# Token sums of the seven-product channel mixer made per token tile in the output stage, second weight's rows loaded ahead of hidden group 0

## The chip, the cores and the metric

The kernel runs on one core of one Trainium2 chip. The metric is the device time of one execution in microseconds (us); the kernel before took 1729.72 us (median of three runs, 1728.2 to 1732.3).

## What is computed

One layer of a decoder: a normalised and modulated input goes through one wide projection, two kinds of attention, two up projections that are merged by gates, an output projection with a residual, and then a channel mixer. The change lies in the last two parts. S = 1024 tokens, D = 1024 channels, FF = 4096 hidden units, all in float32:

```
mixed = (sigmoid(m_a) * y_a + sigmoid(m_b) * y_b) @ w_out
h  = h + gate1 * mixed
u2 = rms_norm(h, norm2_g) * (1 + scale2) + shift2
ff = square(relu(u2 @ mlp_w1)) @ mlp_w2
h  = h + gate2 * ff
```

## The kernel before

Every float32 product is made as three products of parts: an operand x is split into a high part (`hi`, line 61, a cast on ScalarE) and the rest (`lo`, line 66, a subtraction on VectorE or GpSimd), and TensorE sums high by high, high by low and low by high. A matmul takes a 128x128 stationary part and 512 moving columns.

**The output stage** (lines 1431 to 1487) goes over eight token tiles t of 128 tokens. `out_mm(t, dh)` makes one half of a tile's 1024 channels with 24 matmuls (line 1441), and VectorE multiplies by the gate row and adds to `acc` (lines 1443, 1444); ScalarE sums squares (1445). `norm2` makes the scale and the normalised tile `hn` (1449, 71 to 75, 1452). `turn2` transposes it (1460, eight pieces of 128 columns), modulates it on ScalarE into `uf` (1463, eight pieces), writes `uf` to DRAM (`u_d`, 1465), and splits it into the mixer's input `mth` and `mtl` (1467, 1468). These two tiles are called `u2h` and `u2l` in the mixer; index 0 holds tokens 0 to 511, index 1 the rest.

**The channel mixer** goes over eight groups of 512 hidden units. Group 0's hidden units are made plainly by `hidden_units(0)`: eight units of 24 matmuls each (line 1525), of which those for th = 1 read the tokens of index 1. Groups 1 to 7 use Strassen's form with seven products instead of eight for both of the mixer's matmuls. `first_units(c)` makes the hidden units of group c by seven products n = 0 to 6 of 24 matmuls each (line 1638); n = 0 and 1 read `u2h[0]` and `u2l[0]`, the five others read a sum of token blocks. These sums T0 to T4 (high and low part, 1 MB each) lie in DRAM as `t_d`, and `stream` (1572) loads them for each group into a `ring` of two slots, which are the two halves of `u2h[1]` and `u2l[1]`. Slot 0 and slot 1 are free once `hidden_units(0)` has read its last unit.

The sums are made by `token_sums`, a generator which `hidden_units(0)` drives one step per unit: it loads four blocks of `u_d` per step (1542), makes t1 (VectorE, 1550), t3 (GpSimd, 1551), t2 (VectorE, 1552) and t4 (GpSimd, 1553), splits the four results (four casts at 61, four subtractions at 66, two of them on each engine), and writes eight parts to `t_d` (1560). Its fifth sum is the plain block (1534, 1535).

`product(c, m)` makes the second matmul's product m of group c from sums of hidden units and sums of `mlp_w2` blocks (lines 1675 to 1684; sums of raw blocks and the second weight's low parts on GpSimd), 24 matmuls at line 1701, and adds into `acc` (1704). Before that, `w2_load` loads four 512 KB rows of `mlp_w2` (1662) and multiplies them by the gate row `grow2` on GpSimd (1663). For group 0 this stands after unit 5 of `hidden_units`, when the sums' pool `tp` has been closed and the pool `mw`, which holds `w2` and the operands, has been opened in its place:

```
        if n == 5:
            gate_row(grow2, 3, 5 * D, px)
            for _ in sums:
                pass
            close(tp)
            mw = pool("mw", "left")
            w2_load(0)
```

All DMAs of these stages are issued by SP, in the order in which they stand. Each engine executes its list in order; a scheduler of the framework has set each list's order from the program, so that work of neighbouring steps is interleaved. `first_units(c + 1)` is interleaved with the seven products of group c.

Of the kernel before, what the change touches and what calls it, by code (L numbers as in the profile page):

```python
# [35 lines left out]
def build(tc, I, out):  # L36
# [49 lines left out]
    oa_d = dr.tile([512, S], F32, name="oa_d")  # L86
    ob_d = dr.tile([512, S], F32, name="ob_d")
    acc_d = dr.tile([4, 128, D], F32, name="acc_d")
    u_d = dr.tile([NK, 128, S], F32, name="u_d")
    t_d = dr.tile([5, 2, 128, 2048], F32, name="t_d")  # L90

    ps = pool("ps", space=PSUM)
# [1362 lines left out]
    def turn2(t, hn):  # L1455
        uf = t4.tile([128, NK, 128], F32, name="uf4", bufs=2)
        for q in range(2):
            p = px()
            for k in range(4):
                nc.tensor.transpose(p[:, k * 128:(k + 1) * 128], hn[:, (q * 4 + k) * 128:(q * 4 + k + 1) * 128], ident)  # L1460
            for k in range(4):
                kk = q * 4 + k
                nc.scalar.activation(uf[:, kk], p[:, k * 128:(k + 1) * 128], AF.Identity,
                                     scale=a2[:, kk:kk + 1], bias=s2[:, kk:kk + 1])
        nc.sync.dma_start(u_d[:, :, t * 128:(t + 1) * 128].rearrange("k p t -> p k t"), uf)
        ts_ = slice((t % 4) * 128, (t % 4 + 1) * 128)
        nc.vector.tensor_copy(u2h[t // 4][:, :, ts_], uf)
        nc.vector.tensor_tensor(u2l[t // 4][:, :, ts_], uf, f(u2h[t // 4])[:, :, ts_], op=OP.subtract)

    u2h, u2l = mth, mtl  # L1470
    wq = pool("wq", "right")
    for t in range(4):
        out_mm(t, 0)
    wo_s[1] = [out_w(k, 1, wq, 4) for k in range(4)]
    late = []
    for t in range(NT):
        if t >= 4:
            out_mm(t, 0)
        out_mm(t, 1)
        late.append((t, norm2(t)))  # L1480
        while len(late) > (2 if t < 4 else 1):
            turn2(*late.pop(0))
    turn2(*late.pop(0))
    close(wq)
    close(gt)
# [10 lines left out]
    w2k = I["mlp_w2"][0]  # L1496
    CH = 4
    NC = FF // 128 // CH
    grow2 = ml.tile([128, D], F32, name="grow2")


    PRODUCTS = (
        (((1, 0, 0),), ((1, 0, 1), (-1, 1, 1)), ((1, 0, 1), (1, 1, 1))),
# [24 lines left out]
            nc.scalar.activation(r, r, AF.Square)  # L1528
            yield


    def token_sums(tp):

        nc.sync.dma_start(t_d[4, 0], f(u2h[1])[:, 4:].rearrange("p k t -> p (k t)"))
        nc.sync.dma_start(t_d[4, 1], f(u2l[1])[:, 4:].rearrange("p k t -> p (k t)"))

        def load(kk):
            X = {}
            for th in range(2):
                for j in range(2):  # L1540
                    X[j, th] = tp.tile([128, 512], F32, name="x%d%d" % (j, th), bufs=2)
                    nc.sync.dma_start(X[j, th], u_d[4 * j + kk][:, th * 512:(th + 1) * 512])
            return X

        X = {kk: load(kk) for kk in range(2)}
        yield
        for kk in range(4):
            b11, b12, b21, b22 = (X[kk][i] for i in ((0, 0), (0, 1), (1, 0), (1, 1)))
            t1 = tp.tile([128, 512], F32, name="t1", bufs=2)
            nc.vector.tensor_tensor(t1, b12, b11, op=OP.subtract)  # L1550
            nc.gpsimd.tensor_tensor(b12, b22, b12, op=OP.subtract)
            nc.vector.tensor_tensor(b22, b22, t1, op=OP.subtract)
            nc.gpsimd.tensor_tensor(b21, b21, b22, op=OP.subtract)
            for n, (src, e) in enumerate(((b22, "v"), (b12, "g"), (b21, "g"), (t1, "v"))):
                h = tp.tile([128, 512], F32R, name="th", bufs=7)
                l = tp.tile([128, 512], F32R, name="tl", bufs=7)
                hi(h, src, "s")
                lo(l, src, h, e)
                for q, t_ in enumerate((h, l)):
                    nc.sync.dma_start(t_d[n, q][:, kk * 512:(kk + 1) * 512], f(t_))  # L1560
            yield
            if kk + 2 < 4:
                X[kk + 2] = load(kk + 2)

    ring = [(u2h[1][:, q * 4:q * 4 + 4], u2l[1][:, q * 4:q * 4 + 4]) for q in range(2)]
    streams = [(c, n) for c in range(1, NC) for n in range(5)]
# [45 lines left out]
    def first_units(c):  # L1612
# [10 lines left out]
        for n in range(7):  # L1623
            a_prep(*((c, n + 1) if n < 6 else (c + 1, 0)))
            wh, wl = SPL.pop((c, n))
            q = (c - 1) * 5 + n - 2
            bh, bl = (u2h[0][:, n * 4:n * 4 + 4], u2l[0][:, n * 4:n * 4 + 4]) if n < 2 else ring[q % 2]
            if n == 0:
                R = [pd(), pd()]
            if n in (1, 5):  # L1630
                B = [pt(), pt()]
            bank = R if n in (0, 2, 3, 4) else B
            on = n in (2, 3, 4, 6)
            for ft in range(2):
                fs = slice(ft * 128, (ft + 1) * 128)
                for k in range(4):
                    for m, (a, b) in enumerate(((wh, bh), (wh, bl), (wl, bh))):
                        nc.tensor.matmul(bank[ft], a[:, k, fs], b[:, k], start=(k == 0 and m == 0 and not on),  # L1638
                                         stop=(k == 3 and m == 2), skip_group_check=on)
                if n in (0, 2, 3):  # L1640
                    t = r_tile()
                    nc.scalar.copy(t, bank[ft])
                    (c11, None, u2_, u3_)[n].append(t)
                elif n == 4:
                    t = H[c][2 + ft, 0] = r_tile()
                    act(t, bank[ft])
                else:
                    t = {1: c11, 5: u3_, 6: u2_}[n][ft]
                    nc.vector.tensor_tensor(t, t, bank[ft], op=OP.add)
                    act(t, t)  # L1650
                    H[c][{1: (ft, 0), 5: (2 + ft, 1), 6: (ft, 1)}[n]] = t
            if n >= 2:
                stream(q + 2)
            if 3 <= n < 6:
                a_load(c + 1, n - 3)
            yield

    def w2_load(c, js=range(4)):

        for j in js:  # L1660
            t = W2[c][j] = mw.tile([128, D], F32, name="w2", bufs=4)
            nc.sync.dma_start(t, w2k[(c * CH + j) * 128:(c * CH + j + 1) * 128, :])
            nc.gpsimd.tensor_tensor(t, t, grow2, op=OP.mult)  # L1663

    def side_of(terms, block, name, e):

        h = mw.tile([128, 2, 512], F32R, name=name + "h", bufs=2)
        l = mw.tile([128, 2, 512], F32R, name=name + "l", bufs=2)
        if len(terms) == 2:
            (_, i0, j0), (sg, i1, j1) = terms  # L1670
            src = wr.tile([128, D], F32, name="raw", bufs=3)
# [37 lines left out]
    ORDER = (0, 3, 2, 4, 5, 1, 6)  # L1709
    LAST = {(i, j): m for m in ORDER for _, i, j in PRODUCTS[m][2]}  # L1710
    H, W2 = [{} for _ in range(NC)], [{} for _ in range(NC)]
    tp = pool("tp", "left")
    sums = token_sums(tp)
    for n, _ in enumerate(hidden_units(0)):
        next(sums, None)
        if n in (1, 2, 3):
            a_load(1, n - 1)
        if n == 5:
            gate_row(grow2, 3, 5 * D, px)
            for _ in sums:  # L1720
                pass
            close(tp)
            mw = pool("mw", "left")
            w2_load(0)
    a_prep(1, 0)
    for q in range(2):
        stream(q)
    for c in range(NC):
# [3 lines left out]
        for n, m in enumerate(seq):  # L1732
# [3 lines left out]
                ops = operands(c, seq[n + 1])  # L1736
            if n in (4, 5) and c + 1 < NC:
                w2_load(c + 1, range(2 * n - 8, 2 * n - 6))
            product(c, m, cur)
        next(nxt, None)  # L1740
    finish()
# [23 lines left out]
```

## Time and profile before

| What | us |
|---|---|
| median of three runs | 1729.72 |
| profiled execution, whole | 1733.76 |
| its span in the trace | 1732.0 |
| TensorE (PE) busy | 1650.1 |
| VectorE (DVE) busy | 1270.9 |
| GpSimd (POOL) busy | 946.9 |
| ScalarE (ACT) busy | 876.5 |

PE is the busiest engine. A time such as 1127 in this text is microseconds from the span's start. The output stage's matmuls run from 975 to 1068, group 0's hidden units from 1069 to 1116, and the Strassen form starts at 1116. A matmul's listed duration overlaps its neighbour's; what one costs in a row is read from the starts of successive ones.

### The profile page before, as it was taken

What the parts mean: (1) busy time and instruction counts of PE and PEld (TensorE: products, weight loads), DVE (VectorE), ACT (ScalarE), POOL (GpSimd) and SP (SyncE); (2) the same over time, 40 slices, a digit from 0 to 9 for tenths busy, and PEclk for the clock granted to TensorE, in tenths of its full rate; (3) what the DMA queues carried; (4) which work ended last, traced back from release to release, by engine and by line L of the source; (5) the groups of instructions that cost most, each with busy time, mean ns of one, the idle gap of its engine ahead of it and who ended that gap; (6) DMA issues with size and microseconds to landing.
All of it is one profiled execution on the core that took longest, in us unless ns stands there. A gap on an engine that the chain in (4) does not pass through costs nothing.

```text
span 1732.0 us, 25317 instructions
## 1 busy us (share of the span) xinstructions
PE 1650.1 (95%) x8484; PEld 1386.7 (80%) x8484; DVE 1270.9 (73%) x2614; ACT 876.5 (51%) x1898; POOL 946.9 (55%) x837
## 2 busy tenths in 40 slices
PE   5999999999999989999999999949999999999998
PEld 4879888888888867778778888837788888888886
DVE  7598478777777557778564555737898888979887
ACT  6433366666666456766454344524444444444442
POOL 0021143333433377865145200659998898979897
PEclk9999999999999989999999999969999999999999
DMA  9365312111211164441286523974263645637232
GB/s 306 100 181 168 104 47 59 52 54 49 62 48 44 37 194 128 135 110 47 75 299 226 200 81 109 339 304 159 75 266 134 255 154 199 223 118 279 98 146 97
DMA packets 164922, 249.42 MB, mean 144 GB/s; under 512 B 15592, under 2 KB 113592, under 8 KB 155576
## 3 DMA queue, kind: packets, MB, share of 16 engines
q1 hardware_dynamic: 160568, 245.71, 42.7%
q10 hardware_dynamic: 4224, 2.10, 0.4%
q8 instruction: 67, 1.10, 0.3%
q14 instruction: 63, 0.52, 0.1%
HBM read 205.81 MB, written 41.96 MB: 143 GB/s over the span
## 4 chain that ended last, share of the span: by engine, by line
PE 75%; POOL 7%; DMA 6%; DVE 5%; ACT 3%; issue 2%; SPq 1%; POOLq 0%; DVEq 0%; ACTq 0%
PE pd L748 16%; PE psx L1701 10%; PE pd L1638 7%; PE pt L1638 5%; PE px L1441 5%; PE px L1329 5%; PE po L913 4%; PE pt L947 4%; POOL raw L1675 3%; PE po L1701 3%; DMA adraw<-in_ada_w_dram 2%; PE psx L829 2%; PE psx L830 2%; PE px L1525 2%; PE cb L304 1%
## 5 line engine op out<-in xcount | busy, mean ns | idle before, releaser
L1704 DVE TENSOR_TENSOR acc<-acc,psx 128x512 f32<-128x512 f32 x288 | 178.6, 675 | 16.5 <-PE psx L1701 16.2
L748 PE MATMUL pd<-uh,uwh 128*128 128x512 f32 x448 | 181.6, 405 | 0.7 <-ACT zo L1023 0.7
L748 PE MATMUL pd<-ul,uwh 128*128 128x512 f32 x448 | 178.0, 397 | 0.0
L748 PE MATMUL pd<-uh,uwl 128*128 128x512 f32 x448 | 176.9, 395 | 0.0
L66 DVE TENSOR_TENSOR wl<-aw,wh 128x1024 fp32r<-128x1024 f32 x49 | 107.0, 2184 | 75.2 <-ACT wh L61 75.2
L1675 POOL TENSOR_TENSOR raw<-r 128x512 f32<-128x512 f32 x80 | 135.1, 1708 | 26.8 <-ACT r L1616 26.7
L1701 PE MATMUL psx<-wbl,rah 128*128 128x512 f32 x336 | 131.6, 392 | 5.7 <-POOL wbl L1677 4.3
L1701 PE MATMUL psx<-wbh,rah 128*128 128x512 f32 x336 | 130.6, 391 | 1.3 <-DVE acc L1704 1.3
L1701 PE MATMUL psx<-wbh,ral 128*128 128x512 f32 x336 | 130.8, 389 | 0.0
L905 DVE TENSOR_TENSOR tl<-pt,th 128x512 fp32r<-128x512 f32 (+8 forms) x168 | 103.6, 619 | 34.5 <-ACT th L904 33.4
L904 ACT CAST th<-pt 128x512 fp32r<-128x512 f32 (+8 forms) x168 | 88.7, 530 | 60.8 <-PE pt L947 58.8
L1677 POOL TENSOR_TENSOR wbl<-raw,wbh 128x1024 fp32r<-128x1024 f32 x40 | 105.7, 2643 | 18.9 <-ACT wbh L1676 18.9
L886 POOL TENSOR_TENSOR pcx<-pcx,tot 128x64 f32<-128x64 f32 (+7 forms) x32 | 10.5, 329 | 172.2 <-DVE tot L884 95.3
L1663 POOL TENSOR_TENSOR w<-w,grow 128x1024 f32<-128x1024 f32 x32 | 91.9, 2894 | 17.8 <-DMA w<-in_mlp_w_dram 17.8
L63 POOL TENSOR_SCALAR uwh<-uwr 128x512 fp32r<-128x512 f32 x54 | 33.5, 629 | 123.3 <-PE pd L748 96.8
L748 PEld LDWEIGHTS pd<-uh,uwl 128*128 128x128 f32 x448 | 85.0, 190 | 17.8
L1638 PE MATMUL pd<-mth,wh 128*128 128x512 f32 x224 | 88.6, 397 | 9.3 <-DMA mth<-t_d 7.7
L748 PEld LDWEIGHTS pd<-uh,uwh 128*128 128x128 f32 x448 | 85.4, 191 | 14.9 <-ACT zo L1023 1.1
L1676 ACT CAST rah<-raw 128x1024 fp32r<-128x1024 f32 x40 | 41.5, 1051 | 109.8 <-PE po L1701 61.0
L748 PEld LDWEIGHTS pd<-ul,uwh 128*128 128x128 f32 x448 | 85.3, 191 | 13.2
L1638 PE MATMUL pd<-mtl,wh 128*128 128x512 f32 x224 | 88.6, 395 | 6.2 <-DMA mtl<-t_d 6.2
L1638 PE MATMUL pd<-mth,wl 128*128 128x512 f32 x224 | 88.3, 394 | 0.0
(361 smaller groups left out, 5357.9 us busy)
## 6 DMA issues: line engine op xcount, KB each, us to landing
mth<-t_d SPq DMA_DIRECT2D x35, 1024.0 KB, 8.0
mtl<-t_d SPq DMA_DIRECT2D x35, 1024.0 KB, 5.0
w<-in_mlp_w_dram SPq DMA_DIRECT2D x32, 512.0 KB, 6.0
z_d<-zo SPq DMA_DIRECT2D x56, 256.0 KB, 2.0
aw<-in_mlp_w_dram SPq DMA_DIRECT2D x28, 512.0 KB, 4.9
uwr<-in_w_in_dram SPq DMA_DIRECT2D x54, 256.0 KB, 3.0
adraw<-in_ada_w_dram SPq DMA_DIRECT2D x48, 256.0 KB, 3.2
xa<-in_ada_w_dram SPq DMA_DIRECT2D x32, 256.0 KB, 5.9
```

The lines of the kernel that those rows point to most:

```text
L66: (nc.vector if e == "v" else nc.gpsimd).tensor_tensor(dst, src, f(h), op=OP.subtract)
L748: r = nc.tensor.matmul(p, a, b, start=(k == 0 and n == 0), stop=(k == NK - 1 and n == 2))
L904: nc.scalar.copy(th[:rows, :w], p[:rows, :w])
L905: nc.vector.tensor_tensor(tl[:rows, :w], p[:rows, :w], f(th)[:rows, :w], op=OP.subtract)
L1329: nc.tensor.matmul(p, a, b, start=(k == 0 and n == 0), stop=(k == 3 and n == 2))
L1441: nc.tensor.matmul(p, a[:, k, ts_], b[:, k % 2], start=(k == 0 and n == 0), stop=(k == NK - 1 and n == 2))
L1638: nc.tensor.matmul(bank[ft], a[:, k, fs], b[:, k], start=(k == 0 and m == 0 and not on), stop=(k == 3 and m == 2), skip_group_check=on)
L1663: nc.gpsimd.tensor_tensor(t, t, grow2, op=OP.mult)
L1675: nc.gpsimd.tensor_tensor(d, block(i0, j0, s), block(i1, j1, s), op=OP.add if sg > 0 else OP.subtract)
L1677: (nc.vector if e == "v" else nc.gpsimd).tensor_tensor(l.rearrange("p s n -> p (s n)"), src, f(h).rearrange("p s n -> p (s n)"), op=OP.sub ...
L1701: nc.tensor.matmul(p, a[:, s, qs], b[:, s], start=(s == 0 and n == 0), stop=(s == 1 and n == 2))
L1704: nc.vector.tensor_tensor(acc[:, t, ds_], acc[:, t, ds_], p, op=OP.add if sg > 0 else OP.subtract)
```

## The change

The sums are made by blocks of 128 tokens in the output stage: pair b joins tile b (loaded back from `u_d` as one 512 KB tile `ux`, with one buffer) and tile b + 4 (just transposed and still in `uf`). `token_sums(b, ...)` is called at the end of `turn2(b + 4)`, and asks for the next pair's `ux` at its end. Only tiles 0 to 3 are written to `u_d`, in rows of 4 KB. The parts now lie in `t_d` token block by token block, so the five Strassen products that read a sum take a moving operand of four runs of 128 columns, 512 columns apart. The small tiles of the sums lie in the output stage's pool `t4`, and pools `tp` and `mw` are gone: `w2` and the operands live in `ml`. The first weight's raw blocks of group 1 and the four rows of `mlp_w2` for group 0 are asked for ahead of `hidden_units(0)`; their product with `grow2` (`w2_gate`) follows unit 2. The output weight's second half takes one tile of pool `wr`, one of `wx` and two of `wq` instead of four of `wq`.

```
-        nc.sync.dma_start(u_d[:, :, t * 128:(t + 1) * 128].rearrange("k p t -> p k t"), uf)
+        uff = uf.rearrange("p k t -> p (k t)")
+        if t < 4:
+            nc.sync.dma_start(u_d[t], uff)
...
+        if t >= 4:
+            token_sums(t - 4, uff[:, :512], uff[:, 512:])
+    def u_load(b):
+        t = uxs[b] = t4.tile([128, D], F32, name="ux", bufs=1)
+        nc.sync.dma_start(t, u_d[b])
+    def token_sums(b, b12, b22):
+        ux = uxs.pop(b)
+        b11, b21 = ux[:, :512], ux[:, 512:]
+        t1, t2, t3 = (t4.tile([128, 512], F32, name="t%d" % n, bufs=1) for n in (1, 2, 3))
+        nc.vector.tensor_tensor(t1, b12, b11, op=OP.subtract)
+        nc.gpsimd.tensor_tensor(t3, b22, b12, op=OP.subtract)
+        nc.vector.tensor_tensor(t2, b22, t1, op=OP.subtract)
+        nc.gpsimd.tensor_tensor(b21, b21, t2, op=OP.subtract)
+        for n, (src, e) in enumerate(((t2, "v"), (t3, "g"), (b21, "g"), (t1, "v"))):
...
+            hi(h, src, "s")
+            lo(l, src, h, e)
...
+        if b < 3:
+            u_load(b + 1)
-    wo_s[1] = [out_w(k, 1, wq, 4) for k in range(4)]
+    wo_s[1] = [out_w(k, 1, *((), (wx, 4), (wq, 2), (wq, 2))[k]) for k in range(4)]
...
+        if t == 4:
+            u_load(0)
...
+                bs = [[t_.rearrange("p b (k t) -> p b k t", k=4)[:, :, k] for k in range(4)] for t_ in ring[q % 2]]
...
-    tp = pool("tp", "left")
-    sums = token_sums(tp)
+    for n in range(3):
+        a_load(1, n)
+    grow2 = ml.tile([128, D], F32, name="grow2")
+    w2_load(0)
     for n, _ in enumerate(hidden_units(0)):
-        next(sums, None)
-        if n in (1, 2, 3):
-            a_load(1, n - 1)
-        if n == 5:
+        if n == 2:
             gate_row(grow2, 3, 5 * D, px)
-            for _ in sums:
-                pass
-            close(tp)
-            mw = pool("mw", "left")
-            w2_load(0)
+            w2_gate(0)
```

On SP, where group 0 ends, the list before holds the last parts' writes, then ring loads, first-weight loads (`aw`) and the rows `w2`:

```order
L1560 DMA t_d_64<-tl_13385 128x512
L1560 DMA t_d_64<-tl_13373 128x512
L1572 DMA mth1_11521<-t_d_64 128x2048
L1578 DMA aw_13806<-in_mlp_w1_dram 128x4x256
L1560 DMA t_d_64<-tl_13379 128x512
L1572 DMA mth1_11521<-t_d_64 128x2048
L1572 DMA mtl1_11523<-t_d_64 128x2048 x2
L1578 DMA aw_13808<-in_mlp_w1_dram 128x4x256
L1662 DMA w2_13432<-in_mlp_w2_dram 128x1024
L1662 DMA w2_13435<-in_mlp_w2_dram 128x1024
```

The same place after the change:

```order
L1493 DMA t_d_64<-tl_13183 128x512
L1576 DMA aw_13197<-in_mlp_w1_dram 128x4x256
L1576 DMA aw_13199<-in_mlp_w1_dram 128x4x256
L1576 DMA aw_13201<-in_mlp_w1_dram 128x4x256
L1663 DMA w2_13209<-in_mlp_w2_dram 128x1024
L1663 DMA w2_13211<-in_mlp_w2_dram 128x1024
L1663 DMA w2_13213<-in_mlp_w2_dram 128x1024
L1663 DMA w2_13215<-in_mlp_w2_dram 128x1024
L1576 DMA aw_13205<-in_mlp_w1_dram 128x4x256
L1570 DMA mtl1_11523<-t_d_64 128x2048
L1570 DMA mth1_11521<-t_d_64 128x2048
```

The rows `w2` stood behind three ring loads and now stand ahead of the first one, behind the last write of a sum.

On VectorE, from tile 5's split (`mth1`) to the low parts of hidden unit weights (`wl`), the list before:

```order
L1467 CAST mth1_11521<-uf4_12922 128x8x128
L1449 TENSOR_TENSOR rst2_111<-ssq2_110 128x1
L1468 TENSOR_TENSOR mtl1_11523<-uf4_12922,mth1_11521 128x8x128
L72 RECIPROCAL rtm_107<-rtm_107 128x1
L73 SCALAR_TENSOR_TENSOR rtm_107<-rst2_111,rtm_107 128x1
L74 SCALAR_TENSOR_TENSOR rtm_107<-rtm_107 128x1
L75 SCALAR_TENSOR_TENSOR rst2_111<-rtm_107 128x1
L1443 TENSOR_TENSOR h4_12969<-px_12944,grow_11355 128x512
L1452 TENSOR_SCALAR hn_12920<-acc_12311,rst2_111 128x1024
L1444 TENSOR_TENSOR acc_12311<-acc_12311,h4_12969 128x512
L66 TENSOR_TENSOR wl_13073<-raw_13071,wh_13072 128x1024
```

After the change, where pair 1's sums t1 and t2 stand between:

```order
L74 SCALAR_TENSOR_TENSOR rtm_107<-rtm_107 128x1
L1483 TENSOR_TENSOR t1_12979<-uf4_12958,ux_12890 128x512
L75 SCALAR_TENSOR_TENSOR rst2_111<-rtm_107 128x1
L1443 TENSOR_TENSOR h4_13039<-px_13014,grow_11355 128x512
L1485 TENSOR_TENSOR t2_12980<-uf4_12958,t1_12979 128x512
L1452 TENSOR_SCALAR hn_12956<-acc_12311,rst2_111 128x1024
L66 TENSOR_TENSOR wl_13219<-raw_13217,wh_13218 128x1024
L1444 TENSOR_TENSOR acc_12311<-acc_12311,h4_13039 128x512
L66 TENSOR_TENSOR wl_13225<-raw_13223,wh_13224 128x1024
```

Tile 6's normalised tile `hn` moved behind t1, which reads the loaded `ux`, and both weights' low parts moved behind `hn`.

On ScalarE, between tile 4's and tile 5's modulation (`uf4`), the list before:

```order
L1463 ACTIVATE uf4_12834<-px_12844,s2_109,a2_108 128x128 x4
L1445 ACTIVATE h4_12881,ssq2_110<-acc_12311 128x512
L1463 ACTIVATE uf4_12922<-px_12923,s2_109,a2_108 128x128 x4
L1463 ACTIVATE uf4_12922<-px_12932,s2_109,a2_108 128x128 x4
L1445 ACTIVATE h4_12910,ssq2_110<-acc_12311 128x512
```

After the change:

```order
L1463 ACTIVATE uf4_12836<-px_12846,s2_109,a2_108 128x128 x4
L61 CAST th_12864<-t2_12858 128x512
L61 CAST th_12870<-t3_12859 128x512
L61 CAST th_12876<-ux_12768 128x512
L61 CAST th_12882<-t1_12857 128x512
L1445 ACTIVATE h4_12917,ssq2_110<-acc_12311 128x512
L1463 ACTIVATE uf4_12958<-px_12959,s2_109,a2_108 128x128 x4
L1463 ACTIVATE uf4_12958<-px_12968,s2_109,a2_108 128x128 x4
```

Pair 0's four casts came between the two tiles' modulations.

## Rows read from the trace of the kernel before

**Rows 1.** The page's first part: busy us, share of the span, instructions.
```profile
PE 1650.1 (95%) x8484; PEld 1386.7 (80%) x8484; DVE 1270.9 (73%) x2614; ACT 876.5 (51%) x1898; POOL 946.9 (55%) x837
```

**Rows 2.** Stretch, length, busy PE, PEld, DVE, ACT, POOL; clock, DMA share, GB/s.
```profile
1030.00:1068.60 38.60, 38.60 (x190) 32.36 (x190) 21.11 (x40) 17.43 (x48) 0.00 (x0) 1.00 0.23 69
1068.60:1116.00 47.40, 46.90 (x210) 37.94 (x209) 30.27 (x31) 22.98 (x47) 19.69 (x11) 1.00 0.88 297
1116.00:1180.00 64.00, 39.39 (x145) 30.31 (x143) 26.34 (x21) 19.06 (x29) 45.14 (x25) 0.79 0.72 273
1180.00:1260.00 80.00, 77.62 (x336) 62.81 (x337) 73.02 (x84) 35.83 (x50) 76.74 (x40) 1.00 0.37 131
```

**Rows 3.** The same view, stretches of 6 us.
```profile
1130.00:1136.00 6.00, 1.19 (x2) 0.50 (x2) 2.52 (x3) 3.78 (x7) 0.00 (x0) 0.60 0.97 332
...
1142.00:1148.00 6.00, 5.96 (x14) 4.70 (x15) 0.00 (x0) 0.59 (x1) 0.68 (x1) 0.50 1.03 396
```

**Rows 4.** PE's waits from 1060 to 1180: total us, times, longest.
```profile
PE pt L1638 <- DMA mth<-t_d: 8.6, 1, 8.6
PE pd L1638 <- DMA mth<-t_d: 7.7, 1, 7.7
PE pd L1638 <- DMA mtl<-t_d: 6.2, 1, 6.2
```

**Rows 5.** PE's timeline: start, us, instruction, [idle before, what ended it].
```profile
1068.10 1.04 PE L1460 MATMUL px<-ident,hn 128*128 128x128 f32 x8
1075.12 1.09 PE L1460 MATMUL px<-ident,hn 128*128 128x128 f32 x8 [0.50 <-DVE hn L1452]
...
1134.69 1.19 PE L1638 MATMUL pd<-mth,wh 128*128 128x512 f32 x2 [7.67 <-DMA mth<-t_d]
...
1173.92 0.50 PE L1701 MATMUL psx<-wbl,rah 128*128 128x512 f32 x1 [1.15 <-POOL wbl L1677]
```

**Rows 6.** The chain that ended last, in order of time: start, us, what.
```profile
1014.77 5.46 PE px L1441 x24
1020.23 0.87 PE px L1460 x8
```

**Rows 7.** SP's timeline of DMA issues.
```profile
1128.13 0.37 SPq L1572 DMA_DIRECT2D mth<-t_d  x1
...
1133.34 6.19 SPq L1662 DMA_DIRECT2D w<-in_mlp_w_dram  x4
```

**Rows 8.** GpSimd's timeline.
```profile
1096.48 1.74 POOL L66 TENSOR_TENSOR tl<-x,th 128x512 fp32r<-128x512 f32 x1
...
1123.15 2.86 POOL L1610 TENSOR_TENSOR aw<-aw 128x1024 f32<-128x1024 f32 x1
...
1147.33 10.39 POOL L1663 TENSOR_TENSOR w<-w,grow 128x1024 f32<-128x1024 f32 x4 [17.43 <-DMA w<-in_mlp_w_dram]
```

**Rows 9.** VectorE's timeline.
```profile
1063.46 0.74 DVE L1452 TENSOR_SCALAR hn<-acc,rst 128x1024 f32<-128x1024 f32 x1
...
1064.72 1.22 DVE L66 TENSOR_TENSOR wl<-raw,wh 128x1024 fp32r<-128x1024 f32 x1
...
1096.99 2.31 DVE L66 TENSOR_TENSOR wl<-raw,wh 128x1024 fp32r<-128x1024 f32 x1
...
1103.17 1.77 DVE L66 TENSOR_TENSOR tl<-x,th 128x512 fp32r<-128x512 f32 x1
...
1108.31 0.68 DVE L66 TENSOR_TENSOR tl<-t,th 128x512 fp32r<-128x512 f32 x1
```

**Rows 10.** ScalarE's timeline, tiles 4 and 5.
```profile
1048.56 2.90 ACT L1463 ACTIVATE uf<-px,s,a 128x128 f32<-128x128 f32 x8 [1.08 <-PE px L1460]
...
1056.96 2.90 ACT L1463 ACTIVATE uf<-px,s,a 128x128 f32<-128x128 f32 x8 [0.25 <-PE px L1460]
```

**Rows 11.** DMAs on `u_d`: its writes, then all of them; us to landing.
```profile
u_d<-uf SPq DMA_DIRECT2D x4, 512.0 KB, 3.2
...
DMA to landing us min/median/max: 2.8/5.4/8.4
```

## What the change was forecast to do

> **What bounds the kernel now.** I read the busy times first, then the stages, then PE's waits, then the queues behind the longest waits. PE is busy for 95% of the span [rows 1], so time can be won only where it idles or runs slowly. The stretches show where: PE is full in the output stage (38.60 of 38.60 us) and in group 0's hidden units (46.90 of 47.40), and nearly full again from 1180 on (77.62 of 80), but from 1116 to 1180 it works 39.39 of 64 us, at a mean granted clock of 0.79 [rows 2]. Three waits of 8.6, 7.7 and 6.2 us, each on a load of a token sum [rows 4], and one of 1.15 on the second weight's low part `wbl` [rows 5] make 23.6 us of that gap.
>
> Behind them is one queue. The first ring load is issued at 1128.13 [rows 7], right behind the last writes of sums; the two products that need no sum ended at 1134.69 - 7.67 = 1127.0 [rows 5]. The rows `w2` are issued from 1133.34 [rows 7], behind 5 MB of ring and `aw` loads, with the DMA engines full (0.97 to 1.03, 332 to 396 GB/s, [rows 3]); GpSimd, idle for 17.43 us, starts the gate products only at 1147.33 [rows 8]. So two things are late together: the sums for PE, and `w2` for GpSimd.
>
> What this place costs: from 1127.0 to 1173.92, where the last of the four waits ends [rows 5], PE's list has 75 matmuls (counted in the order). A run of 24 takes 5.46 us [rows 6], so one takes 0.2275 and 75 take 17.1 of 46.9 us. **29.8 us are lost**: 23.6 of waits and 6.2 of slow matmuls. The clock stood at 0.60 and 0.50 in the stretches from 1130 and 1142 [rows 3], mostly the 1.2 GHz level, after PE had idled. So a chain of waits here costs about a quarter more than its length.
>
> **The change part by part.** *The matmul count* does not change, and PE's lists are the same from group 2's part on, so what is won before that point stays won.
>
> *The sums in the output stage.* A pair costs what one step did before: two VectorE and two GpSimd subtractions, four casts, four low parts, eight writes. Reads fall from 16 DMAs of 256 KB to four of 512 KB, writes of `u_d` from eight to four. With one `ux` buffer, a pair's load starts when the pair before has its last low part on GpSimd. I walk this on the old clock. Tile 4's modulation on ScalarE ends at 1051.5, and tile 5's began at 1056.96 [rows 10]. Now pair 0's casts and a sum of squares stand ahead of it, and that sum of squares waits for an `acc` update on VectorE, which stands behind pair 0's t1, t2 and a low part, some of it slowed by GpSimd. I put that update at 1058.9 and the modulation at 1059.7 to 1062.6, 2.7 later than before.
>
> VectorE then makes tile 5's split and a few small operations, about 3 us in all: 1065.5. Its t1 needs pair 1's `ux`. Pair 0's last part on GpSimd is done about 1058.7 (four operations of 1.74 [rows 8] after 1051.5), the issue comes about 1059.4, and a 512 KB transfer in this stage lands in 3.2 us [rows 11]: 1062.7, so the load hides behind the late modulation. t1, the gate product and t2 (0.68 each) and `hn` (0.74, [rows 9]), with gaps, end at 1068.5; PE wants `hn` at 1068.1 [rows 5]: **0.4 of wait**.
>
> *The weights.* The output weight's second half now sits in the buffer that a hidden unit's weight needs, and both low parts `wl` come behind `hn`. A `wl` takes 1.22 alone and 2.31 while GpSimd works, a 512-column one 0.68 and 1.77 [rows 9], and GpSimd is then making pair 1's sums. `wl`, `acc`, `wl` take 3.1 alone and 6.4 beside it. I take 5.5, since GpSimd stops before the last one ends: 1074. PE starts hidden unit (1, 0) at 1069.5 and needs it two matmuls later, at 1070: **4.0 of wait** (1.6 if nothing interferes).
>
> The Trainium skill, "SBUF — State Buffer", section "SBUF: two separate sides", speaks against moving this work here: a VectorE operation with two SBUF inputs and a GpSimd operation that reads SBUF take one port pair as an exclusive lock, and the loser is blocked for the whole instruction. By that page each of the three could wait up to GpSimd's 1.74 in place of the 1.09 between the rows, an estimate of 1.9 us more on this term; the sum goes by the rows.
>
> *Tile 7.* Its `hn` comes after ScalarE's casts of pair 1, tile 6's modulation (2.90) and VectorE's split of tile 6: about 1080.5, and PE is done with unit (1, 0) at 1079.0. **1.5 of wait**, where 0.5 stands now [rows 5]. Tile 7's split, behind pair 2's t1 and t2, is ready about when PE starts the units of th = 1. The hidden units thus end 0.4 + 4.0 + 1.5 - 0.5 = **5.4 us later**: the old end is 1127.0 less 48 matmuls, 1116.0, the new one 1121.4.
>
> *The end of the sums.* Only pairs 0 and 1 fall inside the output stage. Pair 2's low parts end about 1088.5, behind tile 7's modulation; pair 3's `ux` lands at 1092.3, and its t1, t2, t4, cast and two low parts on GpSimd end at 1099.4. This lies beside the hidden units. SP then issues three `aw` and the four `w2`. 2 MB up to the first `w2` take 5 to 6 us at 332 to 396 GB/s [rows 3]; with up to 3 us for the way, GpSimd starts its gates at 1108, not 1147. The gates take 10.39 [rows 8], the work from there to the first `wbl` took 1173.9 - 1157.7 = 16.2, and an `aw` difference of 2.86 now stands inside [rows 8]: first `wbl` at 1137.5.
>
> PE meanwhile: the 48 matmuls without a sum end at 1132.3. The ring loads wait only for the last hidden unit; slot 0's 2 MB take 5 to 6 us and both slots 10 to 12, against 10.9 and 16 until they are needed. In the new list 28 further matmuls stand before the first `wbl`: 1138.7. So **no wait there** (2 us if `w2` lands three later). In the old list 47 more matmuls stood before that point, 10.7 us, so PE would be at the old mark of 1173.9 at 1149.4.
>
> **Sum:** 29.8 - 5.4 = 24.4 us; the walk gives 1173.9 - 1149.4 = 24.5. The profiled execution took 1733.76, which becomes 1709.3. The median of the runs lies 4.0 below it; the waits belong to one stage of every run, so I take the same 24.5 off the median: 1705.2, **1705**.
>
> *The moving operand in four runs.* 840 matmuls (five of seven products, 24 each, seven groups) now read four runs of 128 columns. No row of before has this form. Bounds: one instruction over 512 columns is 0.2275; four separate ones over 128 are 4 x 0.87 / 8 = 0.435 [rows 6]. It can't go below 0.2275, since the same columns stream. It stays one instruction, so I take the near end, nothing; the far end is 840 x 0.207 = 174 us.
>
> **The rivals.** *More waits in the output stage.* The landing of `ux` decides. Transfers of `u_d` took 5.4 in the middle and 8.4 at most where the queue was full [rows 11], against the 3.2 that I took. Pair 1's load stands before tile 6's `hn`, pair 2's before tile 7's split. Two loads 2 to 5 us late, or waits long enough to pull the clock down as at 1130 [rows 3], cost 4 to 11 us more: 1709 to 1716. For it: SP's list is in order, with about ten part writes ahead of each load. Against: the DMA engines were used for only 0.23 of 1030 to 1068 [rows 2].
>
> *No new waits.* VectorE and GpSimd hardly meet, the weights come in time, and most of the 2.4 us that PE idles from 1180 to 1260 [rows 2] go too: 29.8 and up to 2.4 off, 1697 to 1700.
>
> *The wait changes its name.* If the chain of single `ux` buffers runs some 25 us longer, so that GpSimd starts its gates at 1133, the first `wbl` comes as late for PE as the sums did: 1727 to 1733. Each pair would need twice the 10 to 12 us of my walk.
>
> *Slower.* The four-run operand costs each of the 840 matmuls more than 24.5 / 840 = 0.029 us, 13%. At 0.04 the kernel is 33.6 - 24.5 = 9 us slower, 1739. For it: the form stands nowhere in the trace, and 0.435 is its far end. Against: columns and instructions are as many as before.
>
> **How the numbers follow.** Forecast (1701 to 1709) 0.60; more waits 0.15; no new waits 0.12; changed name 0.05; four-run operand 0.08. A difference within 0.2%, 3.5 us, is about what a measurement here can't tell from no change. Faster 0.87 (the first three), same 0.05, slower 0.08. The range of 1697 to 1716 holds the first three but for their edges, about 8 in 10.
>
> **What would show it.** Right: PE's waits on `mth` and `mtl` from `t_d` are gone; after group 0's hidden units the clock stays at 1.00; GpSimd starts its gates near 1108, and the first `wbl` lands within 2 us of PE's need; PE waits 5 to 6 us in all between 1068 and 1085, most of it on a `wl`; matmuls on the four-run operand start 0.2275 apart. Wrong: PE idle for over 8 us around the output stage, a wait of over 4 us on `wbl`, or more than 0.24 between those matmuls.

## The result, and the profile after

The changed kernel takes **1712.7 us** (median of four runs, 1710.4 to 1715.7) against 1731.0 before (the three runs of the forecast's 1729.72 and a fourth of 1732.55): a ratio of 0.9891, 95% interval 0.9875 to 0.9908. In two later series it took 1710.8 (0.9873, 0.9856 to 0.9891) and 1713.1 (0.9885, 0.9872 to 0.9899), so it is 18 to 22 us faster. One execution of the kernel before in the first of these series took 4396 us and is left out. The forecast was 1705, 24.5 us faster, with a range of 1697 to 1716: right in its sign and within its range, 3 to 6 us short in the gain. All three medians lie outside the forecast's own bracket of 1701 to 1709, in the one that stood for more waits in the output stage.

The first part of the page of the changed kernel, to be held against [rows 1]:

```profile
span 1709.3 us, 25308 instructions
...
PE 1646.8 (96%) x8484; PEld 1384.8 (81%) x8484; DVE 1276.9 (75%) x2614; ACT 875.7 (51%) x1898; POOL 948.8 (56%) x837
```

PE's work is the same; the span is 22.7 us shorter. Next the stretches, with the columns of [rows 2]:

```profile
1030.00:1068.60 38.60, 38.58 (x191) 31.93 (x189) 28.02 (x44) 21.50 (x54) 11.32 (x7) 1.00 0.38 131
1068.60:1090.00 21.40, 16.52 (x66) 12.66 (x67) 17.46 (x21) 10.20 (x27) 10.95 (x7) 0.92 0.83 257
...
1122.00:1160.00 38.00, 34.92 (x143) 27.35 (x142) 23.38 (x22) 16.33 (x23) 38.00 (x22) 0.96 0.49 185
1138.00:1145.00 7.00, 6.83 (x24) 5.16 (x23) 1.96 (x2) 5.01 (x8) 7.00 (x5) 0.78 0.54 157
1180.00:1260.00 80.00, 79.35 (x347) 64.46 (x346) 69.55 (x75) 34.19 (x48) 71.97 (x37) 1.00 0.50 190
```

The hole of 24.6 us between 1116 and 1180 is gone. Two small ones stand in its place: 4.9 us at the end of the output stage (1068.6 to 1090) and 3.1 us after the hidden units (1122 to 1160), where GpSimd is busy all the time. From 1180 to 1260 PE idles 0.65 us instead of 2.4. PE's waits from 970 to 1300 (total us, times, longest), all of them:

```profile
PE px L1556 <- DVE wl L66: 4.5, 1, 4.5
PE psx L1705 <- ACT wbh L1680: 1.5, 1, 1.5
PE pd L1639 <- DVE wl L66: 0.8, 1, 0.8
PE pd L1639 <- ACT wh L61: 0.6, 1, 0.6
PE psx L1705 <- DVE acc L1708: 0.4, 1, 0.4
PE px L1460 <- DVE hn L1452: 0.4, 1, 0.4
PE psx L1705 <- POOL wbl L1681: 0.2, 1, 0.2
```

None of the three waits on a sum in [rows 4] is left. What set the time in this part is told by the chain that ended last (start, us, what):

```profile
1074.99 6.49 DMA ux<-u_d
...
1089.26 4.73 DMA ux<-u_d
...
1098.95 2.81 DMA t_d<-tl
...
1102.57 3.17 DMA t_d<-tl
...
1106.15 8.88 DMA w<-in_mlp_w_dram
...
1127.56 8.25 POOL raw L1679 x5
...
1140.64 5.71 POOL wbl L1681 x2
...
1221.24 4.22 PE psx L1705 x16
```

It runs through the reload of `ux`, the last writes of the sums, the landing of `w2` and then GpSimd's whole path to `wbl` and on, and reaches PE only at 1221.24. In the kernel before, the chain, as the profile infers it, runs through the same place:

```profile
1137.41 13.64 DMA w<-in_mlp_w_dram
...
1152.03 5.68 POOL w L1663 x2
1157.71 9.01 POOL raw L1675 x5
...
1171.54 4.69 POOL wbl L1677 x2
...
1244.32 3.93 PE psx L1701 x16
```

So GpSimd's path behind the landing of `w2` was the last to arrive before, too; the three waits on sums lay beside it, and at `wbl` PE still waited 1.15. From tile 4's transposes to the point where the chain reaches PE, at neighbouring matmuls of both lists, it took 196.4 us before and takes 174.4: 22.0 less, about the whole gain.

GpSimd's gates and PE's arrival at `wbl`, from their timelines:

```profile
1112.62 12.74 POOL L1667 TENSOR_TENSOR w<-w,grow 128x1024 f32<-128x1024 f32 x4 [11.81 <-DVE aw L1595]
```
```profile
1046.84 1.03 PE L1460 MATMUL px<-ident,hn 128*128 128x128 f32 x8
...
1121.05 0.39 PE L1639 MATMUL pd<-mth,wh 128*128 128x512 f32 x1
...
1144.04 0.50 PE L1705 MATMUL psx<-wbl,rah 128*128 128x512 f32 x1 [0.17 <-POOL wbl L1681]
```

The `aw` that the first row names is VectorE's semaphore; its last needed work, `grow2`, was done before 1106, and the chain shows that the gates waited for `w2`.

**A clock for comparing.** The first row of that fence is tile 4's transposes. They start at 1047.92 before and, in the profiles of this study, anywhere from 1042.67 to 1048.94, though nothing ahead of the output stage differs. So single times scatter by some 6 us for reasons that the change doesn't touch. I therefore count from that row: **D** is the time from it to the end of the span. D is 684.1 before and 662.5 after, 21.6 us less; two further profiles of the changed kernel gave 662.9 and 663.1. From the second matmul of group 2's third product on (1226.9 in the changed kernel), PE's lists of all kernels here agree, and what is left takes 482.1 to 482.6 us in every profile but e2's (484.3): the differences lie ahead of it.

### The profile page after: what moved, and what is told of

Its sections match the earlier page's. It is cut to its first block, busy times and chain, and to the rows that moved or that the text cites. A ratio compares the mean times of both kernels' runs of the same rounds, so it can differ in the third digit from the quotient of the medians.

```text
span 1709.3 us, 25308 instructions
## 1 busy us (share of the span) xinstructions
PE 1646.8 (96%) x8484; PEld 1384.8 (81%) x8484; DVE 1276.9 (75%) x2614; ACT 875.7 (51%) x1898; POOL 948.8 (56%) x837
## 4 chain that ended last, share of the span: by engine, by line
PE 75%; POOL 7%; DVE 6%; DMA 5%; ACT 3%; issue 3%; SPq 0%; POOLq 0%; DVEq 0%; ACTq 0%
PE pd L748 16%; PE psx L1705 10%; PE pd L1639 7%; PE pt L1639 5%; PE px L1329 5%; PE po L913 5%; PE px L1441 4%; PE pt L947 4%; PE po L1705 3%; POOL raw L1679 3%; DMA adraw<-in_ada_w_dram 2%; PE psx L829 2%; PE psx L830 2%; PE po L1180 1%; POOL wbl L1681 1%
## 5 line engine op out<-in xcount | busy, mean ns | idle before, releaser
L66 DVE TENSOR_TENSOR wl<-aw,wh 128x1024 fp32r<-128x1024 f32 x49 | 115.1, 2349 | 65.8 <-ACT wh L61 65.8
L1679 POOL TENSOR_TENSOR raw<-r 128x512 f32<-128x512 f32 x80 | 131.3, 1659 | 32.1 <-ACT r L1614 32.0
```

The source lines that it names most:

```text
L66: (nc.vector if e == "v" else nc.gpsimd).tensor_tensor(dst, src, f(h), op=OP.subtract)
L1679: nc.gpsimd.tensor_tensor(d, block(i0, j0, s), block(i1, j1, s), op=OP.add if sg > 0 else OP.subtract)
```

## The experiments

All times in us; "hidden" is from tile 4's transposes to the first matmul of the Strassen form, where group 0's hidden units end, "gates" to GpSimd's first gate product, "wbl" to the first matmul that reads a `wbl`, "ahead" the number of matmuls that PE's list has between the hidden units' end and `wbl`.

| Kernel | median | ratio to before, 95% | D | hidden | gates | wbl | ahead |
|---|---|---|---|---|---|---|---|
| before | 1731.0 | | 684.1 | 68.1 | 99.4 | 126.0 | 123 |
| after | 1712.7 | 0.9875 to 0.9908 | 662.5 | 74.2 | 65.8 | 97.2 | 76 |
| a0, again | 1710.8 | 0.9856 to 0.9891 | 662.9 | 74.8 | 66.3 | 97.7 | 76 |
| a1, third | 1713.1 | 0.9872 to 0.9899 | 663.1 | 74.5 | 66.5 | 97.9 | 76 |
| e1, w2 late | 1714.6 | 0.9881 to 0.9912 | 666.1 | 77.5 | 68.9 | 100.5 | 76 |
| e1b, the same | 1715.6, one run | | 666.1 | 75.7 | 67.7 | 99.2 | 76 |
| e2, no gates | 1705.0 | 0.9821 to 0.9868 | 661.4 | 77.3 | none | 86.1 | 39 |
| e3, no reload | 1712.5 | 0.9869 to 0.9900 | 663.1 | 81.3 | 65.3 | 90.2 | 32 |
| e4, pair 1 off GpSimd | 1710.4 | 0.9854 to 0.9897 | 661.2 | 77.6 | 63.7 | 94.3 | 61 |
| e5, before, no gates | 1727.8 | 0.9976 to 0.9997 | 681.3 | 68.1 | none | 118.6 | 100 |
| e6, w2 first | 1709.6 | 0.9858 to 0.9891 | 661.7 | 74.4 | 61.8 | 95.0 | 61 |
| e7, gates split | 1710.4 | 0.9855 to 0.9895 | 660.1 | 74.1 | 66.0 | 93.9 | 63 |
| e8, fourth tl | 1713.2 | 0.9871 to 0.9898 | 665.1 | 76.8 | 68.0 | 99.4 | 76 |
| e9, three edits | 1715.8 | 0.9866 to 0.9901 | 665.6 | 76.8 | 63.3 | 88.1 | 29 |

D comes from one profile each, and three of the unaltered kernel differ by 0.6; the medians by 2.4. The last column says where the scheduler set PE's list anew; times to `wbl` compare only where it agrees.

**My theory** was: the sums, which stood in the queue in front of the ring loads, carry the gain; what now arrives last is GpSimd's path (`w2` lands, gates, sums of raw blocks, `wbl`). **Rivals**: the early rows `w2` carry half of the gain; PE's wait of 4.5 on `wl` is what is lost.

### Which half of the change pays: e5 and e1

e5 is the kernel before without group 0's gates:

```
-            nc.gpsimd.tensor_tensor(t, t, grow2, op=OP.mult)
+            if c:
+                nc.gpsimd.tensor_tensor(t, t, grow2, op=OP.mult)
```

> The kernel before, with group 0's four products of w2 and the gate row left out on GpSimd (10.39 us), so that group 0's second weight lacks its gate. Theory, two things late together: the waits of 8.6, 7.7 and 6.2 us on the sums stay, only the last, 1.15 on wbl, goes: 0 to 1.5 us faster than the kernel before. Rival, by which GpSimd's late gates carry the loss and the early rows the gain: about 10 us faster.

Measured: 2.4 us faster by the ratio of 0.9986 (the medians, 1727.8 against 1732.0 in that series, say 4.2), D 2.8 less. PE's waits, and where GpSimd starts on group 0's second weight:

```profile
PE pd L1638 <- DMA mth<-t_d: 7.3, 1, 7.3
PE psx L1702 <- ACT wbh L1677: 7.1, 1, 7.1
PE pd L1638 <- DMA mtl<-t_d: 6.2, 1, 6.2
PE psx L1702 <- POOL wbl L1678: 3.6, 1, 3.6
...
1149.87 1.98 POOL L1676 TENSOR_TENSOR raw<-w,w 128x512 f32<-128x512 f32 x1 [20.12 <-DMA w<-in_mlp_w_dram]
```

With 10.4 us of GpSimd's work gone, PE still stands for 24 us: 13.5 on two sums, and 10.7 on parts of the second weight, since product 0 now comes earlier in the list (100 matmuls ahead of `wbl`, not 123). Those parts hang on the rows `w2`, which land as late as before: GpSimd waits 20.12 us for them. So less work on GpSimd alone returns little, somewhat more than I expected and far below the rival's 10. What the rows alone would bring if they came early, e5 doesn't show.

e1 is the changed kernel with `w2` late:

```
-    w2_load(0)
     for n, _ in enumerate(hidden_units(0)):
-        if n == 2:
+        if n == 5:
             gate_row(grow2, 3, 5 * D, px)
+            w2_load(0)
             w2_gate(0)
```

> The rows w2 of group 0 and their product with the gate row stand after unit 5, as in the kernel before; the sums stay in the output stage. Theory: the sums were what the three long waits hung on, but the gates start some 10 us later and GpSimd's path (rows land, gates, sums of raw blocks, wbl) is already the last one to arrive at n = 2, so PE waits 5 to 9 us longer at the first wbl or at the operands of n = 2: 1717 to 1723. Rival: the sums alone make the gain, and w2 has time enough either way: 1711 to 1715, no difference.

Measured: 1714.6, 3.9 above the yardstick of the same series, whose expectation was this:

> The changed kernel once more, unaltered, as the yardstick for the others of this job: 1711 to 1715 us. In its trace the wait on wl of unit (1, 0) is 4.5 us, and three waits on low parts and casts between 1132 and 1138 make 2.9 us; both theories expect these again.

D is 3.0 to 3.6 longer. So the rows' place in the program is worth some 3 us, less than the theory's 5 to 9 and more than the rival's nothing. But in time the rows hardly moved: on tile 4's clock SP issues the first of them at 61.6, against 57.7 to 58.4 in the changed kernel and 85.4 before, and the gates started only 1.3 to 3.1 us later. With the sums' writes gone from the middle of the hidden units, SP reaches the rows soon from either place; in the changed kernel it waits there 0.6 for a last write of a sum. So e1 doesn't separate early sums from early rows. Moving the sums brought both, and how the gain divides between the two no run here shows. The chain of the kernel before speaks against the sums alone: with `w2` landing as late as there, GpSimd would have had the first `wbl` no sooner.

### Does GpSimd's path set the time: e2

```
         if n == 2:
             gate_row(grow2, 3, 5 * D, px)
-            w2_gate(0)
```

> Group 0's four products of w2 with the gate row are left out on GpSimd, so the second matmul of group 0 uses weights without their gate; nothing else is changed. Theory: the waits on wl, wh and wbh between 1132 and 1138 and the slow clock behind them hang on GpSimd's gates (12.74 us): they go, 3.1 us of waits and 2.6 of slow matmuls, about 5.7 us faster than the changed kernel. Rival: these waits come from the order on VectorE and ScalarE alone: no difference.

Measured: 1705.0, 5.7 below the yardstick's 1710.8. All its waits from 1036 to 1300, and one stretch of 6 us after the hidden units, beside the same stretch of the changed kernel (second block):

```profile
PE px L1460 <- DVE hn L1452: 6.1, 1, 6.1
PE px L1556 <- DVE wl L66: 1.2, 1, 1.2
PE psx L1705 <- DVE acc L1708: 0.6, 1, 0.6
...
1134.00:1140.00 6.00, 6.00 (x28) 4.99 (x27) 4.04 (x7) 0.28 (x1) 6.00 (x4) 1.00 0.37 126
```
```profile
1134.00:1140.00 6.00, 3.79 (x11) 2.66 (x12) 1.86 (x3) 4.12 (x6) 6.00 (x4) 0.81 0.08 20
```

The waits on `wh`, `wl`, `wbh` and `wbl` at n = 2 are gone, and the clock stays at 1.00. From the hidden units' end on it took 584.1 against 588.0 to 588.6, though PE reads the first `wbl` 37 matmuls earlier. In its profile the output stage was 2.5 to 3.1 us longer, so D fell by 1.1 to 1.7 only; the profiled run was the longest of its five. The rest, from 1225.6 on, took 1.9 us more than in the changed kernel's profiles, with a wait of 0.94 for `acc` at 1417, far behind the gates. Without these two, from the hidden units' end to where the lists agree again, it took 99.8 us against 105.7 to 106.3: 6 us less, as the theory had it. The medians say the same, but the two intervals overlap, and the list is set anew, so the order of the lists has a share that isn't separated.

The same is seen without leaving work out. Six profiles have 76 matmuls ahead of `wbl`: after, a0, a1, e1, e1b and e8. In all of them `wbl` is read 31.3 to 31.5 us after the gates start, while the gates' start moves by 3.1 us and the hidden units' end by 3.3. From the hidden units' end to `wbl` it is 22.6 to 23.5 us, less constant, but the two points move together in these six, so this alone is weak; the chain above, which runs through GpSimd, and e2 are the stronger signs that PE's arrival follows GpSimd.

### The output stage: e4, and one kernel profiled twice

e4 takes pair 1's four operations off GpSimd:

```
-        nc.gpsimd.tensor_tensor(t3, b22, b12, op=OP.subtract)
+        if b != 1:
+            nc.gpsimd.tensor_tensor(t3, b22, b12, op=OP.subtract)
...
-            lo(l, src, h, e)
+            if b == 1 and e == "g":
+                l = h
+            else:
+                lo(l, src, h, e)
```

> Pair 1's four GpSimd operations (two subtractions, two low parts) are left out; the casts' results are written in the low parts' place, so the sums of this token block are wrong. It tells whether wl is late through GpSimd beside VectorE. Theory: wl, acc, wl take about 3.1 us instead of 6.3, the wait of PE on wl falls from 4.5 to about 1.2; as GpSimd's path at n = 2 is the next to arrive and doesn't start from here, the time falls by only 0 to 1.5 us. Rival 1: the time falls by the whole 3.3. Rival 2: the three take 6.3 us as before, the wait stays at 4.5 (VectorE's own list, not the other engine): no difference.

Measured: 1710.4, no difference, D 1.3 to 1.9 less. `wl`, `acc`, `wl` took 3.0 us and PE's wait on `wl` fell to 0.9, as the theory had it. But VectorE's list came out in another order too, and PE waited 7.3 us for `hn` of tile 7, so its waits there grew in sum from 4.9 to 8.2. The time that fits the theory's 0 to 1.5 us therefore doesn't refute rival 1.

What happens without any edit is clearer. In e1 and e2 GpSimd lost in the place where VectorE loses in the changed kernel. The yardstick of the last series and e1 once more were to tell whether the program or the execution decides:

> The changed kernel a third time, unaltered: yardstick of this job, 1707 to 1715 us. It also bears on one question. Beside pair 1's sums VectorE and GpSimd met in two ways so far: in both profiles of the changed kernel VectorE lost (its wl, acc, wl took 6.3 us, GpSimd's subtraction into ux 1.67), in the kernel with w2 late and in the one without the gates GpSimd lost (5.15 us, and VectorE's three 3.1), though their lists are the same up to there. If each execution decides anew, this profile shows one or the other; if the program decides, VectorE loses again.

> The kernel with w2 and its gates after unit 5 once more, unaltered, for the same question. If the program decides which engine loses beside pair 1's sums, GpSimd's subtraction takes 5.2 us again, PE waits over 6 us for hn of tile 7, and from tile 4's transposes to the end it takes 666 us again. If each execution decides, VectorE may lose this time: then PE waits 4.5 us on wl as in the changed kernel, and the difference to it from tile 4 on (662.5 to 662.9) is the price of the late w2 alone, which I put at 2 to 4 us.

The same code, e1 and then e1b, GpSimd's timeline and VectorE's (start, us, instruction):

```profile
1068.48 5.16 POOL L1486 TENSOR_TENSOR ux<-ux,t 128x512 f32<-128x512 f32 x1 [3.62 <-DVE t L1485]
...
1068.92 1.22 DVE L66 TENSOR_TENSOR wl<-raw,wh 128x1024 fp32r<-128x1024 f32 x1
1070.06 0.69 DVE L1444 TENSOR_TENSOR acc<-acc,h 128x512 f32<-128x512 f32 x1
1070.66 1.22 DVE L66 TENSOR_TENSOR wl<-raw,wh 128x1024 fp32r<-128x1024 f32 x1
1071.80 0.69 DVE L66 TENSOR_TENSOR tl<-t,th 128x512 fp32r<-128x512 f32 x1
```
```profile
1067.21 1.67 POOL L1486 TENSOR_TENSOR ux<-ux,t 128x512 f32<-128x512 f32 x1 [3.62 <-DVE t L1485]
1068.85 2.24 POOL L66 TENSOR_TENSOR tl<-t,th 128x512 fp32r<-128x512 f32 x1
...
1067.66 2.31 DVE L66 TENSOR_TENSOR wl<-raw,wh 128x1024 fp32r<-128x1024 f32 x1
1069.89 1.74 DVE L1444 TENSOR_TENSOR acc<-acc,h 128x512 f32<-128x512 f32 x1
1071.56 2.28 DVE L66 TENSOR_TENSOR wl<-raw,wh 128x1024 fp32r<-128x1024 f32 x1
```

In e1 GpSimd's subtraction took 5.16 us, through four VectorE operations that ran at full speed; in e1b it took 1.67, and VectorE's three took 6.2. So the program alone doesn't decide it. Nor does the chip alone: e1b ran on another one than e1, but a0, whose lists are the same up to this place, ran on e1's, and there VectorE lost. In e1 PE waits 1.25 on `wl` and then 6.5 for `hn` of tile 7, since pair 1's casts and low parts, which stand ahead of that tile on ScalarE and VectorE, come later; in e1b it waits 4.5, 0.3 and 1.1. Hidden units end 1.9 us apart, and **D is the same, 666.1 and 666.1**. The way there isn't what I expected. GpSimd's gates are 1.2 us apart too, and PE reads `wbl` 1.3 us apart, after a wait of 3.2 in both. The rest goes by the clock: from that read, 16 matmuls took 5.04 us in e1 and 6.24 in e1b, at a granted clock of 0.68 and 0.53.

```profile
1149.40:1154.44 5.04, 5.04 (x16) 4.01 (x16) 3.28 (x5) 0.00 (x0) 5.04 (x3) 0.68 0.99 406
```
```profile
1146.85:1153.09 6.24, 6.24 (x15) 4.90 (x16) 3.60 (x5) 0.00 (x0) 6.24 (x4) 0.53 0.99 395
```

Why the clock came back after 7 matmuls in one and after 13 in the other no run shows, so the equal D is in part luck. Against the rival that the 4.5 on `wl` is the loss stands e3, below: there the hidden units end 6.5 to 7.1 us later, and D is the same. It isn't refuted by a run that takes this wait alone away.

### The reload: e3

```
-            u_load(b + 1)
+            uxs[b + 1] = ux
```

> Pairs 1 to 3 take the tile ux that is already in SBUF in place of a load of their own, so their sums are of wrong blocks; three loads of 512 KB and the waits for them are gone. Theory: VectorE waited 1.32 and 3.43 us for ux, so the sums end 5 to 8 us earlier, w2 and the gates start 3 to 8 us earlier, and the waits between 1132 and 1138 shrink: 2 to 5 us faster than the changed kernel, with the wait of 4.5 on wl left as it is. Rival, by which the landing of ux decides in the output stage: the wait on wl falls to below 2 as well, and 5 to 9 us are won. Third: PE has no wait on ux at all, and nothing changes.

Measured: 1712.5, D 663.1, no difference; the numbers of theory and rival were both wrong. The waits for `ux` were gone and pair 3's last part came 3.4 to 4.1 us earlier, but:

```profile
PE px L1460 <- DVE hn L1452: 9.2, 2, 5.8
...
1113.63 11.36 POOL L1667 TENSOR_TENSOR w<-w,grow 128x1024 f32<-128x1024 f32 x4 [14.67 <-DMA w<-in_mlp_w_dram]
```

With the tile there at once, the scheduler put pair 1's and pair 2's work ahead of `hn` of tiles 6 and 7, and the hidden units end 6.5 to 7.1 us later; and GpSimd still waits for `w2`, whose gates start 65.3 us after tile 4, 0.5 to 1.2 earlier than with the reload. What PE lost more ahead of the hidden units' end it lost less behind it, where its waits fell from 3.1 to 1.0. The landing of `ux` is a part of the chain, but taking it away hardly moves the start of the gates.

### Relieving GpSimd: e6, e7, e8, e9

e6 asks for `w2` ahead of the three `aw` loads; e7 gives two of the four gates to VectorE; e8 gives the low parts a fourth buffer; e9 does all three.

```
+    w2_load(0)
     for n in range(3):
         a_load(1, n)
     grow2 = ml.tile([128, D], F32, name="grow2")
-    w2_load(0)
```
```
-            nc.gpsimd.tensor_tensor(W2[c][j], W2[c][j], grow2, op=OP.mult)
+            (nc.vector if c == 0 and j in (1, 3) else nc.gpsimd).tensor_tensor(W2[c][j], W2[c][j], grow2, op=OP.mult)
```
```
-            l = t4.tile([128, 512], F32R, name="tl", bufs=3)
+            l = t4.tile([128, 512], F32R, name="tl", bufs=4)
```

> The changed kernel with the four rows w2 asked for ahead of the three aw loads of group 1, not behind them; nothing is left out. Theory: the rows land some 4 us earlier, the gates start some 3 us earlier, and of the waits of 3.1 us and the slow clock of 2.6 at n = 2 half goes: 2 to 4 us faster than the changed kernel, if the aw difference on GpSimd does not come later by as much. Rival: SP reaches these issues late in either order, because it stands behind the last sums' writes, and nothing moves: no difference.

> The changed kernel with two of group 0's four products of w2 and the gate row on VectorE; nothing is left out. Theory: GpSimd's path is 5 to 6 us shorter, the waits between 1132 and 1138 and the slow clock go: 3 to 5.7 us faster than the changed kernel. Rival: VectorE, on which those weights' low parts stand too, becomes late by the 2 to 4 us of the two products: the waits stay under another name, no difference or up to 2 us slower.

> The sums' low parts get a fourth buffer tl, nothing else is edited; the scheduler then puts tile 6's hn ahead of pair 1's t1 and t2 between the two wl. Theory: the waits of PE around the output stage come from VectorE's list and from the low parts' buffers, whose writes VectorE waits for (0.3 to 3.7 us each time); so the waits on wl and hn, 4.9 us in the changed kernel, fall to 1 to 3, and from tile 4's transposes to the end it takes 659 to 661 us instead of 662.5 to 662.9. Rival: GpSimd's path to the first wbl decides, and an earlier end of the hidden units is waited away at n = 2: no difference, 662 to 663.

> Three edits together, nothing left out: the fourth buffer tl, the rows w2 ahead of the first weight's loads, and two of the four products with the gate row on VectorE. Singly the two last took 1.0 and 2.6 us off the stretch from tile 4's transposes to the end. Theory: both places that PE waits at are relieved, so the gains add: 656 to 659 us for that stretch, and some 4 to 6 us off the time of the changed kernel. Rival: they relieve one and the same wait in turn, and VectorE is the next to be late: 659 to 661, not to be told from the changed kernel by the time.

e6 moved the gates 3.9 to 4.6 us ahead and gained 0.8 to 1.4 in D; e7 cut them by 6.7 us and gained 2.3 to 3.0. Neither can be told from the changed kernel by its times. The waits of e6 and of e7 after the hidden units:

```profile
PE pt L1639 <- ACT wh L61: 2.0, 1, 2.0
PE pt L1639 <- DVE wl L66: 1.3, 1, 1.3
```
```profile
PE pt L1639 <- DVE wl L66: 2.2, 1, 2.2
PE pt L1639 <- ACT wh L61: 1.1, 1, 1.1
```

PE's waits there are now all for the first weight's parts, which in e6 are loaded later and in e7 stand behind the gates on VectorE: 3.3 us under other names, as e7's rival said of the waits, though not of D.

e8 went the wrong way: D 665.1, 2.0 to 2.7 longer, where I expected 659 to 661. The waits of the output stage were 6.1 instead of 4.9 (1.4 on `wl`, 4.7 on `hn`), and pair 3's `ux` came so late that the gates started at 68.0, with `wbl` 31.4 behind them. e9 started the gates at 63.3 and was no better, 665.6: the scheduler now has the first `wbl` after 29 matmuls instead of 76, and PE waits 3.2 us there. Why its five times lie in two groups, 1709.6 to 1709.9 and 1715.8 to 1716.4, I can't say; its profile is of the longer group. No version that does all the work beats the changed kernel by its times. e6 and e7 together, without the fourth buffer, were not tried.

## Why the prediction was right, and where it was short

- *What was lost before* (29.8 us, two things late together): right. The waits on sums are gone, and the gates start 33.6 us earlier by tile 4's clock. That neither alone would have done is read from the chain of the kernel before and from e5, where 10.4 us less of GpSimd's work returned 2.4; it was not run.
- *The output stage*, 5.4 us: near in its sum, with other parts, so in part by luck. The hidden units end 6.2 to 6.8 us later by tile 4's clock; the wait on `wl` is 4.5 (forecast 4.0), on `hn` of tile 6 nothing (0.4), of tile 7 0.4 (1.5), and the rest is a lower clock after the wait, 0.92 in that stretch. `wl`, `acc`, `wl` took 6.2, as the rows had it (6.4), where I had taken 5.5. The estimate from the Trainium skill, "SBUF — State Buffer", section "SBUF: two separate sides", 1.9 more, did not come: each loses only what is left of the other's operation. But that rule's exclusive lock is seen in e1, where GpSimd lost through four operations in a row.
- *No wait at the first `wbl`*: **the step that failed**. Tile 4's transposes are 1.1 us earlier in this profile; on its clock the walk gave 1098.3 for the last low part, 1106.9 for the gates and 1136.4 for the first `wbl`. They came at 1100.8, 1112.6 and 1144.0. The 7.6 us are 2.5 up to the last low part, behind `ux`, which landed in 5.1, 6.5 and 4.7 us and not in 3.2; 3.2 from there to the gates' start, where the issue of `w2` waited for writes of `tl` and a row took 8.9 us to land; and 2.4 from the gates, 12.74 long and not 10.39, beside VectorE's subtractions of 3.3 to 3.4 each; less 0.4 in the work behind them. PE was due at 1137.6 by the walk, 1138.3 with the longer output stage, and came 5.7 late: 3.1 of waits (0.57, 0.85, 1.49, 0.17) and 2.6 of slow matmuls behind them (clock 0.78 from 1138 to 1145). ScalarE passes the delay on: its cast `rah` waits for GpSimd's raw sums, and the `wh` of n = 2 stands behind it.
- *What was left out of the sum*: PE's smaller waits after 1173.92 before, 3.3 us, went too, but for 0.4 on `acc`. 24.4 - 0.7 - 5.7 + 2.9 = 20.9, and D fell by 21.6; 0.7 is not accounted for. PE's lists agree only from the second matmul of group 2's third product on, not from group 2's start.
- *The moving operand in four runs*: right, it costs nothing. 24 matmuls on it take 5.44 us ([rows 6] has 5.46):

```profile
1226.83 5.44 PE pd L1639 x24
```

- *The rivals*: "more waits in the output stage" named the landing of `ux`, rightly late, but as PE's wait; it worked through GpSimd instead. "The wait changes its name" is what happened on a small scale, 5.7 us in place of the 22 and more that it was priced at.

## What to carry to other kernels

When a queue that several engines wait for is cleared, work out the second-latest path as carefully as the first: take each transfer at the landing time that its neighbours' traffic gives, and each operation at its duration beside the engine it will run next to. Read the chain that ended last as well as the waits: here it named GpSimd's path before the change already, while the longest waits named the sums. A constant distance between two events (here 31.4 us from the gates to `wbl`) tells something only where other distances vary. Where stages ahead scatter by more than the effect, count from an event behind them, and to one where the lists agree again.

## What the runs showed of the hardware that I had not expected

When VectorE and GpSimd meet on two-input operations, either may lose, in two executions of the same program (on two chips): 6.2 us for VectorE's three operations beside a subtraction of 1.67 on GpSimd, or 3.0 beside one of 5.16. In the first case they alternate, and each listed time is about its own plus the rest of the other's operation (1.22 becomes 2.3); in the second VectorE's four operations follow each other without a gap, and GpSimd gets in after the last. What decides it no run here shows.
